# A hybrid decoder layer on one core: the projections' operands at other places in SBUF

## The chip, the cores and the metric

The kernel runs on one core of a Trainium2 chip. The metric is the device time of one execution in microseconds. A core has TensorE (PE in the profile; PEld is its loading of weights), VectorE (DVE), ScalarE (ACT), GpSimd (POOL), SyncE (SP), which here issues nearly all DMAs, and 16 DMA engines. Tiles lie in SBUF, 128 partitions wide; a tile has the same byte address in each partition. A matmul loads a stationary operand of up to 128 columns from SBUF (the LDWEIGHTS of the profile) and then streams a moving operand of up to 512 columns from SBUF, adding into a tile in PSUM. The next matmul's stationary operand is loaded while the current one streams.

## What is computed

One decoder layer for 512 positions of width 1024, in float32, with x and all weights in DRAM:

```python
h = rms_norm(x, norm_w)
u_s, z_s, q, k, v, z_a, r_s, r_a = split(h @ w_in)          # 1024 x 9216
y_s = s5_branch(u_s, ...)                                   # diagonal state space, GELU,
                                                            # gated by sigmoid(g @ w_glu)
y_s = (y_s * silu(z_s)) @ w_ssm_out
y_a = dilated_attention(rope(rms_norm(q)), rope(rms_norm(k)), v)   # 3 groups x 8 heads of 64
y_a = (y_a * silu(z_a)) @ w_attn_out
m = sigmoid(r_s) * y_s + sigmoid(r_a) * y_a
out = x + m @ w_o
```

## The kernel before

**Three products for one.** Every large product is made of operands split in two: hi is the value in the type float32r, lo the rest. `mm3` (L122, its matmuls are L63 in the profile) adds hi x hi, hi x lo and lo x hi into one PSUM tile `pj`, so 128 rows of contraction take three matmuls. Five activations go through it, all transposed (features on the partitions):

- `hT` (L220), the normalized input, [128, 8, 512] in hi and in lo, against all of `w_in`;
- `gT` (L685), the state-space branch after its GELU, against `w_glu`;
- `yT`, the gated branch, against `w_ssm_out`;
- `aT` (L1081), the gated attention, [128, 2, 4, 512], hi and lo in one tile, against `w_attn_out`;
- `mT`, the merged branches, against `w_o`.

**Units.** `load_w` (L185) brings a block of weights of 128 x 1024 by DMA into `w_raw`; ScalarE makes `w_hi` of it (L108) and VectorE `w_lo` (L110). `cm_unit` (L195) takes such a block as stationary operand, in slices of 128 columns, and streams the activation, 512 columns at a time: 8 x 3 = 24 matmuls. `wide_granule` and `tok_granule` do it the other way round: a slice of 128 positions of the activation is stationary, and 512 or 256 columns of weights are moving. The first three blocks are taken with 256 columns of `hT` at a time. A stationary slice is 128 x 4 = 512 bytes, a moving one 2048 or 1024, and every slice starts at a multiple of 512 bytes into its tile. So the distance between a moving and a stationary operand, modulo 512 bytes, is that of their tiles.

**Order.** The work goes through the norm, the projections that feed the state-space branch with that branch's scan between them, `w_glu`, `w_ssm_out`, four rounds of attention (projections of two heads each, scores, softmax, values), `w_attn_out` and `w_o`. Tile pools place the tiles and a planner orders the instructions of each engine.

**Places.** A pool puts its tiles one behind the other in the order in which the program first asks for them, rounded up to 32 bytes. The pool `cst` comes first (`ident`, `nwc`, then `hT_hi` and `hT_lo`), then `wp` with the weights, then `big`, whose tags s4, s7a, s3, s6a, s2, s7b, s1, s5 and s6b are places that several tiles take one after another. The bytes in a partition, before:

| tile (tag) | address | modulo 512 | distance to the weights |
| --- | --- | --- | --- |
| hT_hi, hT_lo | 17056, 33440 | 160 | 32 below |
| w_hi, w_lo (three each) | 74432 to 94912 in steps of 4096 | 192 | 0 |
| gT_lo, aT (s4) | 99008 | 192 | 0 |
| gT_hi (s3) | 120000 | 192 | 0 |
| yT_lo, mT_lo (s2) | 142528 | 192 | 0 |
| yT_hi, mT_hi (s1) | 163008 | 192 | 0 |

The operands of the scores (`qkp`, hi in s1 and lo in s2) are at 192 modulo 512 too.

Of the kernel before, what the change touches and what calls it, by code (L numbers as in the profile page):

```python
# [11 lines left out]
F32 = mybir.dt.float32  # L12
F32R = mybir.dt.float32r
# [7 lines left out]
P = 128  # L21
D = 1024
S = 512
KT = D // P
NB = S // P
G = 64
N = 64
# [6 lines left out]
NP = 4  # L34
NG = 3
# [17 lines left out]
def tile_hybrid_block(ctx: ExitStack, tc: tile.TileContext, x, positions, norm_w, w_in, lam_re, lam_im,  # L53
# [21 lines left out]
    cst = ctx.enter_context(tc.tile_pool(name="cst", bufs=1))  # L75
    wp = ctx.enter_context(tc.tile_pool(name="wp", bufs=3))
    big = ctx.enter_context(tc.tile_pool(name="big", bufs=1))
# [4 lines left out]
    ps_p = ps_first.enter_context(tc.tile_pool(name="ps_p", bufs=3, space=PSUM))  # L82
    ps_g = ps_first.enter_context(tc.tile_pool(name="ps_g", bufs=5, space=PSUM))

    scr_t = big.tile([P, 4096], F32, name="scr", tag="s4")
    scr_o = [0]

    def scr(shape, dtype=F32):
# [11 lines left out]
    def bank(name):  # L100
        return ps_g.tile([P, 512], F32, name=name, tag="g")
# [103 lines left out]
    nw8 = big.tile([KT, P], F32, name="nw8", tag="s7a")  # L205
    act.dma_start(nw8, norm_w[0].rearrange("(k p) -> k p", p=P))
    nwc = cst.tile([P, KT], F32, name="nwc")
    nps = bank("nps")
    pe.transpose(nps[:, 0:KT], nw8, ident[:KT, :KT])
    dve.tensor_copy(nwc, nps[:, 0:KT])  # L210
# [6 lines left out]
        if r in (1, 2):  # L217
            prefetch(len(loaded) + 1)
    lo_w[0] = dve
    hT_hi = cst.tile([P, KT, S], F32R, name="hT_hi")  # L220
    hT_lo = cst.tile([P, KT, S], F32R, name="hT_lo")

    ss = scr([P, NB])
    ms = scr([P, NB])
# [147 lines left out]
    cs = scr([G, N])  # L372
    sincos(sn, cs, th_, [G, N], "la")

    pw = big.tile([G, 2, 9, N], F32, name="pw", tag="s7a")
    dve.tensor_tensor(pw[:, 0, 0], mag, cs, op=ALU.mult)
    dve.tensor_tensor(pw[:, 1, 0], mag, sn, op=ALU.mult)
    den = scr([G, N])
# [13 lines left out]
    dve.tensor_tensor(t2, nr, li, op=ALU.mult)  # L392
    dve.tensor_tensor(t1, t1, t2, op=ALU.subtract)
    dve.tensor_tensor(pw[:, 1, 8], t1, den, op=ALU.mult)
    tq = big.tile([G, 2, 4, N], F32, name="tq", tag="s7b")
    for n in (1, 2, 4):

        br_ = pw[:, 0:1, n - 1:n, :].broadcast_to([G, 2, n, N])
# [1 line left out]
        a = pw[:, :, 0:n, :]  # L400
# [141 lines left out]
    sp.dma_start(qkw[:, 1].rearrange("p g d -> p (g d)"),  # L542
                 k_norm_w[0].rearrange("g d -> (g d)").unsqueeze(0).to_broadcast([P, NG * HD]))
    dve.tensor_scalar(qkw[:, 0], qkw[:, 0], -0.125, None, op0=ALU.mult)
    wcol = cst.tile([P, NG, 2], F32, name="wcol")
    wps = bank("wcp")
    for g in range(NG):
        for a in range(2):
# [50 lines left out]
            act.copy(V[:, 1:3, 2 * b:2 * b + 2], pss[b].rearrange("p (r g c) -> p g r c", r=2, g=2))  # L599

    def new_v():
        return big.tile([P, NG, NB, P], F32, name="V", tag="s6a")


    scn = big.tile([P, 4096], F32, name="scn", tag="s3")
# [61 lines left out]
    V = None  # L667
    fill = list(order)

    def filler():  # L670
        nonlocal V
        kind, c = fill.pop(0)
        if kind == "v0":
            V = new_v()
            v0_unit(0, V)()
        elif kind == "v":
            v_granule(0, V)
        else:
            {"za": za_unit, "zs": zs_unit, "rs": rs_unit, "ra": ra_unit}[kind](c)
# [3 lines left out]
        wx(*js)  # L683

    gT_hi = big.tile([P, KT, S], F32R, name="gT_hi", tag="s3")  # L685
    gT_lo = big.tile([P, KT, S], F32R, name="gT_lo", tag="s4")
    Mb = [dd[:, o:o + 1024].rearrange("p (g k) -> p g k", g=8) for o in (0, 1024, 2048)]
    for M in Mb:
        pool.memset(M, 0.0)
# [206 lines left out]
    def qk_second(hp, mid=None):  # L896

        pss = wide_granule(hT_hi, hT_lo, mid)
        raw = new_raw(0)
        V = new_v()  # L900
        sq = sml.tile([P, NB, 8], F32, name="ssq")[:, :, 0:4]
        for r in range(NB):
            act.copy(raw[:, r], pss[r][:, 0:256])
            squares(sq[:, r], pss[r][:, 0:256])
            act.copy(V[:, 1:3, r], pss[r][:, 256:512].rearrange("p (g c) -> p g c", g=2))  # L905
        qk_norm((2,), [raw], sq)
        return raw, V
# [170 lines left out]
    QK = (QT, KA, KB)  # L1078
    ptb = big.tile([P, 4, 512], F32, name="ptb", tag="s6b")
    PT = [ptb[:, i] for i in range(4)]  # L1080
    aT = big.tile([P, 2, NP, S], F32R, name="aT", tag="s4")  # L1081

    raws = qk_first()

# [9 lines left out]
    for hp in range(NP):  # L1094
        Pt = scores(hp, *QK)
        if hp < NP - 1:
# [12 lines left out]
            V = V_next  # L1109
# [18 lines left out]
    for cc in range(KT // 2):  # L1128
        hi, lo = get_w()
        for c2 in range(2):  # L1130
            c = 2 * cc + c2
# [50 lines left out]
```

## Time and profile before

| | us |
| --- | --- |
| three runs | 736.49, 738.57, 737.64 |
| median | 737.64 |
| profiled execution: span from the first instruction to the last | 732.6 |
| VectorE busy | 457.1 |
| ScalarE busy | 314.6 |
| GpSimd busy | 191.7 |

The profiled execution is given by its span alone; the median of the runs is 5.0 us above it, for what lies before the first and behind the last instruction. The page lists the busy time of each engine, the span in 40 slices, the chain of work that ended last (followed back from the last instruction, at each step to what released it) and groups of instructions by line, engine, operation and tile. A row of such a group ends in the busy time of the group, the mean duration of one in ns, and the idle time of the engine before them. A row of the timeline begins with the start of the instruction and its duration in us; where several alike follow each other they are one row with a count. The durations of matmuls overlap, since a matmul starts before the one ahead of it has drained: the time from one start to the next is what a matmul costs the engine.

### The profile page before, as it was taken

The page shows a single profiled execution, that of the slowest core. Times are in us where ns is not written, and L with a number is a line of the kernel's source. Part 1 is how long each engine was busy: PE and PEld are TensorE (multiplying, and loading weights), DVE is VectorE, ACT ScalarE, POOL GpSimd, SP SyncE. Part 2 cuts the span into 40 slices and gives each one's busy share as a digit, 9 for nine tenths or more (in the row PEclk, how much of TensorE's full clock was granted, in tenths as well). Part 3 has the DMA queues.
Part 4 walks back from the last instruction along what each step waited for, and adds up shares of the span by engine and source line. Part 5 has one row for each costly group of instructions (what it writes and reads, how often), then busy time and mean ns, then how long its engine had stood idle before and what let it go on. Part 6 is the DMA issues. An engine that isn't in the chain of part 4 may idle for free.

```text
span 732.6 us, 12680 instructions
## 1 busy us (share of the span) xinstructions
PE 699.6 (95%) x4821; PEld 574.2 (78%) x4821; DVE 457.1 (62%) x912; ACT 314.6 (43%) x631; POOL 191.7 (26%) x346
## 2 busy tenths in 40 slices
PE   2799899999999999999999999999989999999997
PEld 2687688778878787888888888788868877878886
DVE  6759673989946546764335659655664666464832
ACT  6434463332326465442144456537153734443420
POOL 3426540230205343550000316021601250230000
PEclk9999999999999999999999999999999999999999
DMA  8433653564547554455333432222412231326441
GB/s 203 106 96 94 171 144 77 137 149 132 120 131 153 122 103 133 139 168 172 99 100 87 130 87 79 66 58 58 115 31 79 65 89 30 115 73 236 139 144 57
DMA packets 137213, 82.14 MB, mean 112 GB/s; under 512 B 32696, under 2 KB 125632, under 8 KB 137024
## 3 DMA queue, kind: packets, MB, share of 16 engines
q1 hardware_dynamic: 135088, 78.96, 37.5%
q0 software_dynamic: 2048, 2.36, 2.6%
q8 instruction: 38, 0.62, 0.4%
q14 instruction: 23, 0.19, 0.1%
q10 hardware_dynamic: 16, 0.00, 0.0%
HBM read 68.46 MB, written 10.49 MB: 108 GB/s over the span
## 4 chain that ended last, share of the span: by engine, by line
PE 87%; DMA 4%; ACT 3%; DVE 3%; SPq 2%; issue 1%; ACTq 0%
PE pj L63 71%; DMA w_raw<-in_w_in_dram 3%; PE sps L63 3%; PE yps L63 3%; PE ot L63 2%; PE ptp L67 2%; PE kps L63 2%; PE xps L63 1%; PE qtp L67 1%; DMA Uj<-ud 1%; ACT w_hi L108 1%; SPq L442 1%; PE wps L67 1%; ACT qkp L873 1%; DVE w_lo L110 1%
## 5 line engine op out<-in xcount | busy, mean ns | idle before, releaser
L108 ACT ACTIVATE w_hi<-w_raw 128x1024 fp32r<-128x1024 f32 x100 | 106.0, 1061 | 236.8 <-PE pj L63 206.6
L110 DVE TENSOR_TENSOR w_lo<-w_raw,w_hi 128x1024 fp32r<-128x1024 f32 x98 | 124.3, 1268 | 107.9 <-ACT w_hi L108 107.2
L63 PE MATMUL pj<-hT_lo,w_hi 128*128 128x512 f32 (+1 forms) x344 | 132.9, 387 | 3.0 <-DVE hT_lo L251 3.0
L63 PE MATMUL pj<-hT_hi,w_hi 128*128 128x512 f32 (+1 forms) x344 | 132.8, 389 | 2.4 <-ACT V L905 1.4
L63 PE MATMUL pj<-hT_hi,w_lo 128*128 128x512 f32 (+1 forms) x344 | 132.4, 386 | 1.6 <-DVE w_lo L110 1.6
L63 PE MATMUL pj<-w_hi,hT_hi 128*128 128x512 f32 (+1 forms) x288 | 106.5, 372 | 0.0
L63 PE MATMUL pj<-w_lo,hT_hi 128*128 128x512 f32 (+1 forms) x288 | 106.5, 370 | 0.0
L63 PE MATMUL pj<-w_hi,hT_lo 128*128 128x512 f32 (+1 forms) x288 | 106.0, 371 | 0.0
L63 PEld LDWEIGHTS pj<-hT_lo,w_hi 128*128 128x128 f32 x344 | 66.0, 192 | 16.2 <-DVE hT_lo L251 3.9
L63 PEld LDWEIGHTS pj<-hT_hi,w_hi 128*128 128x128 f32 x344 | 65.5, 192 | 16.5 <-ACT V L905 2.1
L63 PEld LDWEIGHTS pj<-hT_hi,w_lo 128*128 128x128 f32 x344 | 65.9, 192 | 15.4 <-DVE w_lo L110 2.3
L63 PEld LDWEIGHTS pj<-w_hi,hT_hi 128*128 128x128 f32 x288 | 54.1, 188 | 10.0 <-issue 0.2
L63 PEld LDWEIGHTS pj<-w_hi,hT_lo 128*128 128x128 f32 x288 | 54.0, 188 | 10.0
L63 PEld LDWEIGHTS pj<-w_lo,hT_hi 128*128 128x128 f32 x288 | 54.0, 188 | 9.8
L931 ACT ACTIVATE Pt<-Pt,st 128x256 f32<-128x256 f32 (+1 forms) x64 | 31.0, 492 | 18.7 <-DVE st L929 18.7
L735 POOL TENSOR_TENSOR kt<-kt,dg 16x128 f32<-16x128 f32 x8 | 4.6, 571 | 125.0 <-ACT kt L734 118.4
L852 POOL TENSOR_TENSOR rt<-qraw,tC 128x256 f32<-128x256 f32 x12 | 14.3, 1189 | 87.7 <-DVE qraw L846 87.4
L739 POOL DMA_DIRECT2D dd<-kt x64 | 33.7, 535 | 2.4 <-POOL kt L735 2.4
L874 DVE SCALAR_TENSOR_TENSOR qkp<-qtp,wcol,qkp 128x512 fp32r<-128x512 f32 (+1 forms) x32 | 23.0, 745 | 13.5 <-ACT qkp L873 13.4
L961 POOL COPY sw<-st 32x4 f32<-32x4 f32 x64 | 12.0, 187 | 73.2 <-ACT Pt L931 70.5
L873 ACT ACTIVATE qkp<-qtp,wcol 128x512 fp32r<-128x512 f32 (+1 forms) x32 | 20.8, 685 | 15.7 <-PE qtp L67 10.4
L277 POOL TENSOR_TENSOR ab<-dd,AT 128x512 f32<-128x512 f32 x16 | 23.0, 1446 | 11.6 <-DVE ab L278 11.6
(263 smaller groups left out, 1289.4 us busy)
## 6 DMA issues: line engine op xcount, KB each, us to landing
w_raw<-in_w_in_dram SPq DMA_DIRECT2D x40, 512.0 KB
w_raw<-in_w_in_dram SPq DMA_DIRECT2D x112, 128.0 KB
w_raw<-in_w_glu_dram SPq DMA_DIRECT2D x8, 512.0 KB
w_raw<-in_w_ssm_out_dram SPq DMA_DIRECT2D x8, 512.0 KB
w_raw<-in_w_o_dram SPq DMA_DIRECT2D x8, 512.0 KB
x_all<-in_x_dram SPq DMA_DIRECT2D x4, 512.0 KB
ud<-uT SPq DMA_DIRECT2D x8, 256.0 KB
Uj<-ud SPq DMA_DIRECT2D x8, 256.0 KB
```

What stands on the lines that cost most here:

```text
L63: last[0] = nc.tensor.matmul(*a, **k)
L67: last[0] = nc.tensor.transpose(*a, **k)
L108: act.activation(hi, src, AF.Copy, scale=scale)
L110: e.tensor_tensor(lo, src, hi.bitcast(F32), op=ALU.subtract)
L277: eng.tensor_tensor(tv, a2.unsqueeze(2).broadcast_to(sh), ai, op=ALU.mult)
L442: sp.dma_start(D1[64 * h:64 * h + 64, a], bv[a][h])
L739: pool.dma_start(M[Q * t:Q * t + Q, :, 0:P - Q * t], kt[:, :, t:].rearrange("q g k p -> q g (k p)"))
L852: pool.tensor_tensor(t1, rh[:, :, :, 0:16], cv.broadcast_to([P, NB * 2, 2, 16]), op=ALU.mult)
L873: act.activation(hi, ps[sl], AF.Copy, scale=w)
L874: dve.scalar_tensor_tensor(lo, ps[sl], w, hi.bitcast(F32), op0=ALU.mult, op1=ALU.subtract)
L931: act.activation(o, o, AF.Exp, bias=nm, scale=-1.0, accum_out=st[:, kind, 1, h, b:b + 1])
L961: pool.tensor_copy(sw[32 * r:32 * r + 32, :, :, b], st[32 * b:32 * b + 32, 1, :, :, r])
```

## The change

No operation is added, removed or put elsewhere in the program. `wcol`, a tile of 24 bytes in `cst`, is asked for ahead of `hT_hi` and not behind `maskB`; so `hT` begins 32 bytes higher and all that follows in `cst` ends where it did. In `big` the tiles of four tags ask for 128, 128, 64 and 64 bytes more (s4, s7a, s6a, s7b); those of s4 use what lies behind the first 128 bytes, the others leave the end unused. So the places behind them move up.

```diff
+    def offset(shape, dtype, name, tag, pad):
+
+        n = int(np.prod(shape[1:]))
+        v = big.tile([P, pad + n], dtype, name=name, tag=tag)[:, pad:]
+        if len(shape) == 3:
+            v = v.rearrange("p (a b) -> p a b", b=shape[2])
+        elif len(shape) == 4:
+            v = v.rearrange("p (a b c) -> p a b c", b=shape[2], c=shape[3])
+        return v
+
-    scr_t = big.tile([P, 4096], F32, name="scr", tag="s4")
+    scr_t = offset([P, 4096], F32, "scr", "s4", 32)
...
     nwc = cst.tile([P, KT], F32, name="nwc")
+    wcol = cst.tile([P, NG, 2], F32, name="wcol")
+    hT_hi = cst.tile([P, KT, S], F32R, name="hT_hi")
+    hT_lo = cst.tile([P, KT, S], F32R, name="hT_lo")
...
-    pw = big.tile([G, 2, 9, N], F32, name="pw", tag="s7a")
+    pw = big.tile([G, 2 * 9 * N + 32], F32, name="pw", tag="s7a")[:, 0:2 * 9 * N].rearrange("g (a k n) -> g a k n", a=2, k=9)
...
-    tq = big.tile([G, 2, 4, N], F32, name="tq", tag="s7b")
+    tq = big.tile([G, 1024 + 16], F32, name="tq", tag="s7b")[:, 0:512].rearrange("g (a k n) -> g a k n", a=2, k=4)
...
-        return big.tile([P, NG, NB, P], F32, name="V", tag="s6a")
+        return big.tile([P, NG * NB * P + 16], F32, name="V", tag="s6a")[:, 0:NG * NB * P].rearrange("p (g b c) -> p g b c", g=NG, b=NB)
...
-    gT_lo = big.tile([P, KT, S], F32R, name="gT_lo", tag="s4")
+    gT_lo = offset([P, KT, S], F32R, "gT_lo", "s4", 32)
...
-    aT = big.tile([P, 2, NP, S], F32R, name="aT", tag="s4")
+    aT = offset([P, 2, NP, S], F32R, "aT", "s4", 32)
```

The places that follow from these sizes:

| tile (tag) | address | modulo 512 | distance to the weights |
| --- | --- | --- | --- |
| hT_hi, hT_lo | 17088, 33472 | 192 | 0 |
| w_hi, w_lo | as before | 192 | 0 |
| gT_lo, aT (s4) | 99136 | 320 | 128 |
| gT_hi (s3) | 120256 | 448 | 256 |
| yT_lo, mT_lo (s2) | 142848 | 0 | 320 |
| yT_hi, mT_hi (s1) | 163392 | 64 | 384 |

The other tiles of `big`, and the pools `tmp` and `sml` behind it, move by 64 to 384 bytes. The operands of the scores lie 64 bytes modulo 512 apart between hi and lo.

More of the change, by code (lines that the diff above doesn't have):

```diff
@@ L219, in tile_hybrid_block @@
     lo_w[0] = dve
-    hT_hi = cst.tile([P, KT, S], F32R, name="hT_hi")
-    hT_lo = cst.tile([P, KT, S], F32R, name="hT_lo")
     ss = scr([P, NB])
@@ L544, in tile_hybrid_block @@
     dve.tensor_scalar(qkw[:, 0], qkw[:, 0], -0.125, None, op0=ALU.mult)
-    wcol = cst.tile([P, NG, 2], F32, name="wcol")
     wps = bank("wcp")
```

## The prediction

> **What bounds the kernel now.** I read the page first, from the busy times to the chain of work that ended last.
>
> ```profile
> span 732.6 us, 12680 instructions
> PE 699.6 (95%) x4821; PEld 574.2 (78%) x4821; DVE 457.1 (62%) x912; ACT 314.6 (43%) x631; POOL 191.7 (26%) x346
> PEclk9999999999999999999999999999999999999999
> PE 87%; DMA 4%; ACT 3%; DVE 3%; SPq 2%; issue 1%; ACTq 0%
> ```
>
> TensorE is busy for 95% of the span, at practically its full granted clock, and 87% of the chain is its own work. So the end of the kernel moves with the time from one matmul's start to the next one's. The chain's shares by line and the window of all instructions that touch the tile pj say which matmuls those are:
>
> ```profile
> by line: PE pj L63 71.3%; DMA w_raw<-in_w_in_dram 2.6%; PE sps L63 2.6%; PE yps L63 2.6%; PE ot L63 2.1%; PE ptp L67 1.9%; PE kps L63 1.7%; PE xps L63 1.3%; PE qtp L67 1.0%; DMA Uj<-ud 1.0%; ACT w_hi L108 0.9%; SPq L442 0.9%; PE wps L67 0.9
> 0.00:733.00 733.00, 576.83 (x2568) 457.43 (x2568) 24.35 (x36) 64.28 (x138) 0.99 0.41 112
> ```
>
> In the second row stand the window, its length, then busy time and (count) of TensorE. The 2568 projection matmuls (pj) are 71.3% of the chain. The groups of TensorE kept apart by shape count them by operand. Each row is one of three products that mm3 issues, except aT, whose row and the one after it hold two and one:
>
> ```profile
> L63 PE MATMUL pj<-hT_hi,w_hi 128*128 128x512 f32 x296 | 118.8, 401 | 1.4 <-ACT V L905 1.4
> L63 PE MATMUL pj<-w_hi,hT_hi 128*128 128x512 f32 x224 | 88.6, 398 | 0.0
> L63 PE MATMUL pj<-gT_hi,w_hi 128*128 128x512 f32 x64 | 24.7, 391 | 1.0 <-ACT gs L776 1.0
> L63 PE MATMUL pj<-yT_hi,w_hi 128*128 128x512 f32 x64 | 24.9, 389 | 0.0
> L63 PE MATMUL pj<-w_hi,mT_hi 128*128 128x512 f32 x64 | 24.4, 389 | 0.0
> L63 PE MATMUL pj<-aT,w_hi 128*128 128x512 f32 x64 | 19.9, 393 | 0.0
> L63 PE MATMUL pj<-w_hi,hT_hi 128*128 128x256 f32 x64 | 18.0, 281 | 0.0
> L63 PE MATMUL pj<-aT,w_lo 128*128 128x512 f32 x32 | 12.4, 392 | 0.0
> L63 PE MATMUL pj<-hT_hi,w_hi 128*128 128x256 f32 x48 | 14.0, 312 | 1.0 <-ACT w_hi L108 1.0
> ```
>
> So hT takes part in 3 x (296 + 224) = 1560 matmuls of 512 columns and 3 x (48 + 64) = 336 of 256. The other four operands have 3 x 64 x 3 + 96 = 672, all of 512. Their mean durations are 389 to 393 ns, hT's 398 to 401. These durations overlap; what the chain pays is the distance between starts, and the timeline of TensorE gives it. First and last rows of four unbroken runs (hT moving, 15 steps; hT stationary, 15; gT, 15; mT stationary, 15):
>
> ```profile
> 168.07 0.40 PE L63 MATMUL pj<-hT_hi,w_lo 128*128 128x512 f32 x1
> ...
> 171.57 0.40 PE L63 MATMUL pj<-hT_hi,w_lo 128*128 128x512 f32 x1
> ...
> 378.38 0.39 PE L63 MATMUL pj<-w_hi,hT_hi 128*128 128x512 f32 x1
> ...
> 381.88 0.40 PE L63 MATMUL pj<-w_hi,hT_hi 128*128 128x512 f32 x1
> ...
> 305.86 0.39 PE L63 MATMUL pj<-gT_hi,w_lo 128*128 128x512 f32 x1
> ...
> 309.26 0.39 PE L63 MATMUL pj<-gT_hi,w_lo 128*128 128x512 f32 x1
> ...
> 710.11 0.39 PE L63 MATMUL pj<-w_hi,mT_hi 128*128 128x512 f32 x1
> ...
> 713.51 0.39 PE L63 MATMUL pj<-w_hi,mT_hi 128*128 128x512 f32 x1
> ```
>
> With hT 3.50 us / 15 = **233.3 ns**, in either role. With gT and mT 3.40 us / 15 = **226.7 ns**, in either role. Same shape, same type, same clock, no wait between. What differs in the program is the place: before, hT begins 32 bytes off the weights' place modulo 512, and gT, yT, mT and aT begin at it. Every slice of these tiles and of the weights that a matmul takes starts at a multiple of 512 bytes into its tile, so a distance modulo 512 holds for all of a stage's matmuls.
>
> **The change part by part.** No instruction, DMA or wait is added or removed; only addresses move. The weights stay where they are, so no queue gets a new step.
>
> *hT to distance 0.* The nearest row for the new distance is gT's and mT's 226.7 ns. Per matmul 233.3 - 226.7 = 6.67 ns, times 1560 = 10.4 us. Two deductions. First, distance 0 doesn't give 226.7 at once. This is the start of the aT stage, just behind the last hT matmuls:
>
> ```profile
> 655.61 0.63 PE L63 MATMUL pj<-aT,w_hi 128*128 128x512 f32 x2
> 656.08 0.39 PE L63 MATMUL pj<-aT,w_lo 128*128 128x512 f32 x1
> ...
> 656.77 0.39 PE L63 MATMUL pj<-aT,w_lo 128*128 128x512 f32 x1
> ...
> 657.45 0.39 PE L63 MATMUL pj<-aT,w_lo 128*128 128x512 f32 x1
> ...
> 658.13 0.39 PE L63 MATMUL pj<-aT,w_lo 128*128 128x512 f32 x1
> ```
>
> From 655.61 to 656.77 are five gaps, 232 ns each; from 657.45 on it is 226.7 (0.68 / 3). Five gaps at 5.3 ns too much cost 27 ns after each break in the stream. The hT matmuls make 65 units of 24 (1560 / 24), and I take one break per unit, as the chain shows two neighbouring ones here with the state-space work between:
>
> ```profile
> 222.15 7.23 PE pj L63 x31
> 229.38 0.32 PE kps L63 x4
> ...
> 234.33 7.23 PE pj L63 x31
> ```
>
> 65 x 27 ns = 1.7 us, leaving 8.7. Second, what isn't on the chain brings nothing: pj holds 0.713 x 732.6 = 522 us of the chain, and its starts add up to 1560 x 233.3 + 336 x 116.7 + 672 x 226.7 ns = 555 us, so 0.94 of it counts: **8.2 us**. The cover that takes the rest is the wait for weights and for the first stages' data, in the 732.6 - 699.6 = 33 us in which TensorE is idle: there a faster matmul only waits earlier.
>
> *hT's 256-column matmuls.* The timeline of such a run (18 steps) and of one at the kernel's start (9 steps), the granted clock of the latter's window (0.50), and the timeline of ten score matmuls with the row that follows them:
>
> ```profile
> 187.19 0.28 PE L63 MATMUL pj<-w_hi,hT_hi 128*128 128x256 f32 x1
> ...
> 189.29 0.28 PE L63 MATMUL pj<-w_hi,hT_hi 128*128 128x256 f32 x1
> ...
> 36.77 0.41 PE L63 MATMUL pj<-hT_hi,w_hi 128*128 128x256 f32 x1
> ...
> 38.69 0.41 PE L63 MATMUL pj<-hT_hi,w_hi 128*128 128x256 f32 x1
> ```
>
> ```profile
> 36.80:38.60 1.80, 1.80 (x10) 0.50 0.00 0
> ```
>
> ```profile
> 435.82 1.36 PE L63 MATMUL sps<-qkp 128*128 128x256 f32 x10
> 437.02 0.39 PE L63 MATMUL pj<-w_hi,hT_hi 128*128 128x512 f32 x1
> ```
>
> They step at 2.10 / 18 = 116.7 ns. At distance 0 the trace has only the scores (sps), ten in 1.20 us, 120 ns; half of the 512-column gap would be 113.3. Bounds 336 x (-3.4 to +3.3 ns), -1.1 to +1.1 us; I take 0.
>
> *gT, yT, mT, aT away from distance 0.* The new distances are 128 (aT, gT_lo), 256 (gT_hi), 320 (yT_lo, mT_lo) and 384 (yT_hi, mT_hi). No row shows these. The best end is a column per clock. Half clock shows 1.92 us / 9 = 213.3 ns for 256 columns, so full clock would give 213.3 for 512: 672 x 13.4 ns = 9.0 us gained. The worst end among the rows is the first pair of aT, 655.61 to 656.08, 235 ns each: 672 x 8.3 = 5.6 us lost. Between them I take **0**. 512- and 256-column matmuls with hT carry the same surcharge per column (20 ns on 213.3, 10 ns on 106.7), which looks like a stall that recurs every few columns, so like a short period in the address. 32 bytes off costs, and the new distances are all multiples of 64. Cover there is none: these stages are pure TensorE, and any loss or gain is paid whole.
>
> *Everything else that moves* (the score operands, now 64 bytes apart between hi and lo; the scan's, tmp and small tiles): the sps share of 2.6% bounds it to well under 1 us either way; taken as 0.
>
> The Trainium skill speaks against the first term. Its page "TensorE: Matmul & The Clock Gate", section "Step-by-step: what each phase is for", says that TensorE reads moving operand and weights through two independent SBUF ports, so that loading the next weights takes nothing from the running matmul. By that the sum would be 0 and the time 737.6. The trace doesn't agree, as far as 233.3 and 226.7 ns can tell. The same page's section "Back-to-back issue gap" gives N / 2.4 + 2.5 ns, an estimate of 215.8 for 512 columns; no row here reaches it, and if the new distances did, the four operands would gain an estimated 7.3 us.
>
> Sum: -10.4 + 1.7 + 0.5 (off the chain) + 0 + 0 = -8.2 us. The span would be 732.6 - 8.2 = 724.4. Against the median of the three runs, 737.64, which lies 5.0 above the span for what is around it, that gives **729.4 us**.
>
> **The rivals.**
>
> 1. *The place isn't why hT is slower.* For: the kernel has one hT only, so tile and place can't be told apart. Against: hT costs 233.3 as moving and as stationary operand, and both hi and lo, as a place would. Time: 737.6. Chance 0.07.
> 2. *Distance 0 is special, and the four others now pay what hT paid.* For: 32 bytes off cost 6.67 ns, and the other distances are unseen. Against: the short period. 672 x 6.67 = 4.5 us back: 733.9. Chance 0.22.
> 3. *Some new distance is better than 0.* For: 226.7 is still 13.4 above the 213.3. Half of that on all four operands: 4.5 us more, 724.9. Chance 0.12.
> 4. *Slower.* The two streams meet at one of the new distances at every fetch, where at distance 0 they soon slip past each other (232 falling to 226.7). From a gap of 226.7 + 8.2 us / 672 = 239 ns on, the four operands eat the gain, and from 242 it is a measurable loss. At three times the surcharge of distance 0, 213.3 + 40 = 253.3 ns, they lose 17.9 us: 747.3. Against: no steady or passing gap in these rows exceeds 235. Chance 0.05.
>
> **How the numbers follow.** The forecast, hT at 226.7 and the others unchanged, has 0.54. A measurement of this kernel tells about 0.3% (2.2 us) from no change, so faster means under 735.4. All of the forecast, rival 3 and most of rival 2 are faster: 0.83. Rival 1 and the worse part of 2 are within: 0.12. Rival 4 is slower: 0.05. The range leaves out rival 4, rival 1 and the extreme of rival 3: from 723, where half the possible gain of the four others meets the whole 256-column one, to 735.5, where they pay 235 ns.
>
> **What would show it.** In the changed kernel's timeline hT's unbroken runs step by 226.7 ns; if they stay at 233.3, rival 1 holds. The gaps of gT, yT, mT and aT, read by hi and lo, decide between the forecast and rivals 2 to 4, each at its own distance. The 256-column runs step by 113 to 120. The chain's share of pj falls while the waits for w_lo and Uj grow by under 1 us. The forecast is wrong if the order of instructions differs, or if idle time of TensorE grows by more than that.

## The result: 5.8 us less

| | median, us | lowest to highest | runs |
| --- | --- | --- | --- |
| before | 736.28 | 734.70 to 738.57 | 7 |
| changed | 730.48 | 729.30 to 733.67 | 7 |

The ratio is 0.992, with a 95% interval of 0.9901 to 0.994: 4.4 to 7.3 us less. The forecast was 729.4.

The page of the changed kernel shows its slowest execution of the seven (own time 733.67, span 731.9):

```profile
span 731.9 us, 12680 instructions
PE 698.2 (95%) x4821; PEld 577.0 (79%) x4821; DVE 454.6 (62%) x912; ACT 314.6 (43%) x631; POOL 189.8 (26%) x346
PEclk9999899999999999999999999999999999999999
PE 89%; ACT 3%; DMA 3%; SPq 2%; DVE 2%; issue 0%; ACTq 0%
```

The 8 in the row of the granted clock goes with its being the slowest: its mean clock is 0.988, that of the other six 0.992 or 0.993, and their spans are 727.5 to 728.9. So a total of this page isn't held against one of before's page; the distances between starts are, read where the clock is full. The number of instructions is the same on every engine, and TensorE's come in the same order.

The timeline of the changed kernel gives those distances (start, duration, instruction). First and last rows of unbroken runs: hT moving, 15 steps; hT's 256 columns, 21; gT, 15; mT, 15; aT, 12:

```profile
158.37 0.39 PE L63 MATMUL pj<-hT_hi,w_hi 128*128 128x512 f32 x1
...
161.77 0.39 PE L63 MATMUL pj<-hT_hi,w_hi 128*128 128x512 f32 x1
...
187.94 0.28 PE L63 MATMUL pj<-w_hi,hT_hi 128*128 128x256 f32 x1
...
190.46 0.28 PE L63 MATMUL pj<-w_hi,hT_hi 128*128 128x256 f32 x1
...
305.99 0.39 PE L63 MATMUL pj<-gT_hi,w_hi 128*128 128x512 f32 x1
...
309.46 0.40 PE L63 MATMUL pj<-gT_hi,w_hi 128*128 128x512 f32 x1
...
709.84 0.39 PE L63 MATMUL pj<-w_hi,mT_hi 128*128 128x512 f32 x1
...
713.29 0.39 PE L63 MATMUL pj<-w_hi,mT_hi 128*128 128x512 f32 x1
...
674.98 0.39 PE L63 MATMUL pj<-aT,w_lo 128*128 128x512 f32 x1
...
677.77 0.39 PE L63 MATMUL pj<-aT,w_lo 128*128 128x512 f32 x1
```

hT steps by 3.40 / 15 = 226.7 ns, its 256 columns by 2.52 / 21 = 120.0; gT by 3.47 / 15 = 231.3, mT by 3.45 / 15 = 230.0 and aT by 2.79 / 12 = 232.5. So hT got what the four others had, and the four others got most of what hT had. Over all unbroken starts (gaps under 250 ns, or 128 for 256 columns) the means in ns are these; they include the first matmuls behind a break:

| matmuls | before | changed | hT alone moved | the four alone moved |
| --- | --- | --- | --- | --- |
| hT, 512 columns (1560) | 233.2 | 227.9 | 227.7 | 233.2 |
| hT, 256 columns (336) | 117.3 | 119.8 | 119.8 | 117.6 |
| gT (192) | 226.8 | 231.4 | 227.0 | 229.3 |
| yT (192) | 226.7 | 231.6 | 226.7 | 232.2 |
| mT (192) | 226.7 | 230.2 | 226.7 | 230.3 |
| aT (96) | 227.3 | 232.5 | 227.0 | 232.5 |

The last two columns belong to the first experiments.

### The profile page after: what moved, and what is told of

Read it like the earlier page. It is cut to its first block, busy times and chain, and to the rows that moved or that the text cites. A ratio compares the mean times of both kernels' runs of the same rounds, so it can differ in the third digit from the quotient of the medians.

```text
span 731.9 us, 12680 instructions
## 1 busy us (share of the span) xinstructions
PE 698.2 (95%) x4821; PEld 577.0 (79%) x4821; DVE 454.6 (62%) x912; ACT 314.6 (43%) x631; POOL 189.8 (26%) x346
## 4 chain that ended last, share of the span: by engine, by line
PE 89%; ACT 3%; DMA 3%; SPq 2%; DVE 2%; issue 0%; ACTq 0%
PE pj L63 73%; PE sps L63 3%; PE yps L63 3%; PE ot L63 2%; PE ptp L67 2%; PE kps L63 2%; DMA w_raw<-in_w_in_dram 1%; PE xps L63 1%; DMA Uj<-ud 1%; PE qtp L67 1%; SPq L453 1%; PE wps L67 1%; ACT qkp L883 1%; ACT w_hi L118 1%; DVE w_lo L120 1%; SPq L229 1%
## 5 line engine op out<-in xcount | busy, mean ns | idle before, releaser
L63 PE MATMUL pj<-gT_hi,w_hi 128*128 128x512 f32 x64 | 25.0, 396 | 1.0 <-ACT gs L786 1.0
```

Source lines behind the costliest of these rows:

```text
L63: last[0] = nc.tensor.matmul(*a, **k)
```

## The experiments

**The change in two halves.** Theory: only the distance between a moving and a stationary operand counts, so the two halves have opposite signs. Rival: the halves don't matter by distance, and the gain comes from elsewhere, or from both. Three kernels on one chip, with before at 734.72 (733.13 to 736.24, 11 runs). The changed kernel once more:

> The changed kernel again, beside the next two on the same chip. Distance theory (a matmul's price depends on the distance between moving operand and weights modulo 512 bytes, 0 being the cheapest seen): hT's 512-column gaps 226.7 ns, the other four 230 to 232.5, together 4 us less than before, ratio about 0.994. If the first comparison's 0.992 holds, 730 us.

Only `wcol` and `hT` moved in `cst`; gT, yT, mT and aT stay at distance 0:

```diff
     nwc = cst.tile([P, KT], F32, name="nwc")
+    wcol = cst.tile([P, NG, 2], F32, name="wcol")
+    hT_hi = cst.tile([P, KT, S], F32R, name="hT_hi")
+    hT_lo = cst.tile([P, KT, S], F32R, name="hT_lo")
...
-    hT_hi = cst.tile([P, KT, S], F32R, name="hT_hi")
-    hT_lo = cst.tile([P, KT, S], F32R, name="hT_lo")
...
-    wcol = cst.tile([P, NG, 2], F32, name="wcol")
```

> hT at distance 0, the other four left at distance 0. Distance theory: hT's gaps 226.7 ns, gT, yT, mT and aT 226.7 as before, so the 3 us that the four lost come back: 7 us less than before, ratio 0.990, and 3 us under the changed kernel. Rival (the four stages got slower because of something other than their distance, such as hT's new place): they stay at 230 to 232 and the time equals the changed kernel's.

The other half alone: the changed kernel with this edit taken back, so hT stays 32 below the weights and the four lie at 128 to 384:

> hT left 32 bytes below the weights, the other four moved as in the change. Distance theory: hT's gaps 233.3 ns as before, the four at 230 to 232.5, 3 us more than before, ratio 1.004. Rival (the four gain or lose nothing on the chain): ratio 1.000.

| | median, us | ratio to before | 95% interval |
| --- | --- | --- | --- |
| the whole change | 729.23 (726.76 to 733.90) | 0.9931 | 0.9906 to 0.9955 |
| hT alone | 728.01 (724.35 to 730.56) | 0.9905 | 0.9882 to 0.9928 |
| the four alone | 738.90 (736.49 to 741.52) | 1.0058 | 1.0038 to 1.0079 |

The window of all instructions that touch pj, in this order, one row from each kernel's trace (window, length, TensorE's busy time and count; then the other engines, granted clock, DMA):

```profile
0.00:733.00 733.00, 572.48 (x2568) 458.45 (x2568) 24.37 (x36) 64.27 (x138) 0.99 0.40 112
```

```profile
0.00:733.00 733.00, 570.37 (x2568) 459.23 (x2568) 24.37 (x36) 64.26 (x138) 0.99 0.40 112
```

```profile
0.00:733.00 733.00, 579.35 (x2568) 457.57 (x2568) 24.36 (x36) 64.24 (x138) 0.99 0.40 112
```

Against the 576.83 of before: hT alone -6.46, the four alone +2.52, and the whole -4.35, which is about their sum (-3.94). So one half of the change brings the gain and the other takes back a third or more of it. hT alone is the better kernel by medians, by 1.2 us where 3 were expected, and its interval overlaps that of the whole change.

**Which distances cost.** The forecast took the new distances to be free because they are multiples of 64. This kernel (from hT alone) gives every load of weights another place, in steps of 32 bytes over 512, hi and lo alike, so all distances occur in one trace. Two buffers of `tmp` pay for the room.

```diff
-        hi = wp.tile([P, kts, cols], F32R, name="w_hi", tag="w_hi")
-        lo = wp.tile([P, kts, cols], F32R, name="w_lo", tag="w_lo")
+        o = 8 * (n_load[0] % 16)
+        n_load[0] += 1
+        hi, lo = (wp.tile([P, 1024 + 128], F32R, name=t, tag=t)[:, o:o + 1024].rearrange("p (k c) -> p k c", k=kts)
+                  for t in ("w_hi", "w_lo"))
```

> All five activations at one place modulo 512, and each block of weights, hi and lo, at 0, 32, 64 ... 480 bytes from it, in turn from load to load; tmp has four buffers instead of six, so only the gaps inside a block of 24 matmuls are read, not the time. Distance theory: each distance has its own steady gap, 226.7 at 0, 230 to 232.5 at 128, 256, 320 and 384, 233.3 where the moving operand lies 32 below (or, with weights moving, 32 above). Rival (only the alignment to 64 bytes matters): two values alone, 226.7 at multiples of 64 and 233.3 at odd multiples of 32.

One execution, 739.29 us. Its timeline in the stage of yT, each row the start of a block of 24 matmuls, with the distance (activation minus weights) falling from 160 by 32 to 0, and the start behind the last block:

```profile
342.01 0.39 PE L63 MATMUL pj<-yT_hi,w_hi 128*128 128x512 f32 x1
...
347.63 0.39 PE L63 MATMUL pj<-yT_hi,w_hi 128*128 128x512 f32 x1
...
353.20 0.40 PE L63 MATMUL pj<-yT_hi,w_hi 128*128 128x512 f32 x1
...
358.80 0.40 PE L63 MATMUL pj<-yT_hi,w_hi 128*128 128x512 f32 x1
...
364.30 0.40 PE L63 MATMUL pj<-yT_hi,w_hi 128*128 128x512 f32 x1
...
369.90 0.39 PE L63 MATMUL pj<-yT_hi,w_hi 128*128 128x512 f32 x1
...
375.34 0.40 PE L63 MATMUL pj<-w_hi,hT_hi 128*128 128x512 f32 x1
```

The blocks take 5.62, 5.57, 5.60, 5.50, 5.60 and 5.44 us, so 234.2, 232.1, 233.3, 229.2, 233.3 and 226.7 ns a matmul for 160, 128, 96, 64, 32 and 0. The means over all blocks with hT moving, without the first six matmuls behind a break or a change of distance and without the last of a block:

| distance | 0 | 32 | 64 | 96 | 128 | 160 | 192 | 224 |
| --- | --- | --- | --- | --- | --- | --- | --- | --- |
| ns | 226.9 | 233.3 | 228.6 | 233.5 | 232.2 | 234.4 | 233.3 | 233.3 |
| distance | 256 | 288 | 320 | 352 | 384 | 416 | 448 | 480 |
| ns | 226.7 | 233.3 | 228.8 | 233.5 | 233.4 | 234.3 | 233.6 | 233.3 |

The second half repeats the first within 0.3 ns, but for 128 and 384 (1.2): the period is 256 bytes. Of these distances 0 and 256 are free, 64 and 320 cost some 2 ns, all others 5 to 8. So neither the short period nor "a multiple of 64" holds: 128 and 192 are multiples of 64 and pay almost all. The expected 230 to 232.5 at 256 and 320 fell too. The sign counts: 64 is cheap and 192, which is -64, is not. The table gives the address of the moving operand minus that of the stationary one. Where hT is stationary the same trace shows the same values (228.4 at 64, 233.3 at 192), so for an activation that is stationary the distance turns round: 320 from the weights counts as 192, and pays.

**Distance or place.** If the place of each operand by itself counted (its alignment, say), hT alone would be fast because 192 modulo 512 is a good place. Here, from hT alone, `wcol` grows so that hT, the weights and the four all move to 288 modulo 512, an odd multiple of 32:

```diff
-    wcol = cst.tile([P, NG, 2], F32, name="wcol")
+    wcol = cst.tile([P, 30], F32, name="wcol")[:, 0:6].rearrange("p (g a) -> p g a", a=2)
```

> hT, the weights and the four others all at one place again, but at 288 modulo 512 (192 in hT_only), an odd multiple of 32. Distance theory: 226.7 ns for all of them and hT_only's time, ratio 0.990. Rival (192 or 448 modulo 512, or a multiple of 64, is a good place in itself): gaps of 233.3 ns, about 15 us more than hT_only, ratio 1.01.

And from hT alone, the four moved by one whole period, to distance 256 (`offset` is the function of the change):

```diff
-    scr_t = big.tile([P, 4096], F32, name="scr", tag="s4")
+    scr_t = offset([P, 4096], F32, "scr", "s4", 64)
...
-    gT_lo = big.tile([P, KT, S], F32R, name="gT_lo", tag="s4")
+    gT_lo = offset([P, KT, S], F32R, "gT_lo", "s4", 64)
...
-    aT = big.tile([P, 2, NP, S], F32R, name="aT", tag="s4")
+    aT = offset([P, 2, NP, S], F32R, "aT", "s4", 64)
```

> hT at distance 0, gT, yT, mT and aT all at distance 256 in hi and lo. Period of 256 bytes, as the probe in steps of 32 showed on hT: gaps of the four 226.7 ns, ratio 0.990 as hT_only. Rival (256 isn't free for these tiles; gT_hi, at 256 in the changed kernel, had 231.5): about 231 ns, 3 us more, ratio 0.994.

On one chip, before at 735.91 (732.02 to 737.65, 11 runs): the first 729.44 us, ratio 0.991 (0.9883 to 0.9936), the second 727.92 us, ratio 0.9892 (0.9868 to 0.9916). An unbroken run of hT in the first and of gT in the second, 15 steps each:

```profile
158.12 0.39 PE L63 MATMUL pj<-hT_hi,w_hi 128*128 128x512 f32 x1
...
161.52 0.39 PE L63 MATMUL pj<-hT_hi,w_hi 128*128 128x512 f32 x1
```

```profile
306.24 0.39 PE L63 MATMUL pj<-gT_hi,w_hi 128*128 128x512 f32 x1
...
309.64 0.39 PE L63 MATMUL pj<-gT_hi,w_hi 128*128 128x512 f32 x1
```

Both 3.40 / 15 = 226.7. The place 288, an odd multiple of 32, is as good as 192 if both operands share it, and 256 is as good as 0. It is the distance that counts. In the changed kernel gT_hi lies at 256, so what gT pays there should come with its lo half at 128. With the four alone moved this can be read off: by the time stamps of that trace, without the first six behind a break, the gap behind a matmul that streams gT_lo is 233.6 ns (62 of them), behind one that streams gT_hi 227.2 (gT_lo streams next) and 226.8 (gT_hi again; 59 each). In the changed kernel, at the same distances, all three are long (230.1, 231.4 and 232.5).

**Below 32 bytes.** The same probe in steps of 4 bytes (`o = 1 * (n_load[0] % 16)`), to see whether distances inside one line of 16 bytes are free:

> All five activations at one place and each block of weights, hi and lo, at 0, 4, 8 ... 60 bytes from it, in turn; tmp has four buffers, so only gaps are read. If what counts is which line of 16 bytes is read, 4, 8 and 12 give 226.7 ns as 0 does, and 16 on 233.3. If 32-byte lines count, up to 28 give 226.7. Rival (any other distance than an exact 0 costs): 233.3 from 4 on. A gap under 226.7 at one of them would be a better place than 0.

One execution, 738.0 us. Timeline, starts of blocks of 24 at distances -4, -8, -12 and -16, and the start behind them:

```profile
155.10 0.39 PE L63 MATMUL pj<-hT_hi,w_hi 128*128 128x512 f32 x1
...
160.68 0.39 PE L63 MATMUL pj<-hT_hi,w_hi 128*128 128x512 f32 x1
...
166.22 0.39 PE L63 MATMUL pj<-hT_hi,w_hi 128*128 128x512 f32 x1
...
171.73 0.39 PE L63 MATMUL pj<-hT_hi,w_hi 128*128 128x512 f32 x1
...
177.33 0.28 PE L63 MATMUL pj<-w_hi,hT_hi 128*128 128x256 f32 x1
```

5.58, 5.54, 5.51 and 5.60 us, so 232.5, 230.8, 229.6 and 233.3 ns. Four bytes off already cost most of the surcharge; the expectation of a free line fell. With the weights moving, +4 gave the highest mean of all, 237.4, while +28 and +60 were nearly free (227.8 and 227.9). No distance of this probe has a mean under 226.7, though single gaps of 225 alternate with 235 at -12.

**Half of the loads displaced.** The 32-byte probe with w_hi left at distance 0 and only w_lo moving (one of every three matmuls uses w_lo):

```diff
-        hi, lo = (wp.tile([P, 1024 + 128], F32R, name=t, tag=t)[:, o:o + 1024].rearrange("p (k c) -> p k c", k=kts)
-                  for t in ("w_hi", "w_lo"))
+        hi, lo = (wp.tile([P, 1024 + 128], F32R, name=t, tag=t)[:, i:i + 1024].rearrange("p (k c) -> p k c", k=kts)
+                  for t, i in (("w_hi", 0), ("w_lo", o)))
```

> The hi half of each block of weights at distance 0, the lo half at 0, 32 ... 480 in turn; tmp has four buffers. In a block with hT moving the three products are (moving hi on w_hi), (lo on w_hi), (hi on w_lo). If the price comes from the loading of the next weights beside the running matmul, the second, during which w_lo is loaded, changes; if it comes from a matmul's own weights, the third. If the matmuls' phases carry over, all three change, and the mean of the three stays between 226.7 and 233.3.

One execution, 737.48 us. Timeline, block starts with hT at the distances 480, 448 and 416 from w_lo (w_lo 32, 64 and 96 bytes further up), and the start behind them:

```profile
159.15 0.39 PE L63 MATMUL pj<-hT_hi,w_hi 128*128 128x512 f32 x1
...
164.74 0.40 PE L63 MATMUL pj<-hT_hi,w_hi 128*128 128x512 f32 x1
...
170.30 0.39 PE L63 MATMUL pj<-hT_hi,w_hi 128*128 128x512 f32 x1
...
175.88 0.39 PE L63 MATMUL pj<-hT_hi,w_hi 128*128 128x512 f32 x1
```

5.59, 5.56 and 5.58 us, so 232.9, 231.7 and 232.5 ns on average, although only a third of the loads is displaced. Which of the three products is long differs by distance: at 384 they take 227, 232.5 and 234 ns, at 480 they take 233, 239 and 228. A displaced third costs nearly as much as displacing all, but this run can't tell which matmul pays, since the next third begins before the stream has settled.

**Which matmul pays.** So, from the kernel just shown, the units that stream an activation over a block of weights (`cm_unit`) are regrouped: first the 16 matmuls with w_hi, then the 8 with w_lo, so that the stream settles within each group. The weights lie 0, 32, ... 224 bytes further up than the activation in turn, w_lo in one kernel and w_hi in its mirror, in which w_lo stays at 0. In this part "at 32" means 32 bytes further up, which is 224 (256 - 32) in the table above.

```diff
-        o = 8 * (n_load[0] % 16)
+        o = 8 * (n_load[0] % 8)
...
         for k in range(kts):
-            mm3(ps, hi[:, k], lo[:, k], rh[:, k], rl[:, k], k == 0, k == kts - 1)
+            pe.matmul(ps, hi[:, k], rh[:, k], start=k == 0, stop=False, skip_group_check=True)
+            pe.matmul(ps, hi[:, k], rl[:, k], start=False, stop=False, skip_group_check=True)
+        for k in range(kts):
+            pe.matmul(ps, lo[:, k], rh[:, k], start=False, stop=k == kts - 1, skip_group_check=True)
```

> In the units that stream the activation over a block of weights the 24 matmuls are regrouped: first the 16 that use w_hi, then the 8 that use w_lo; w_hi lies at distance 0 from the activation, w_lo at 0, 32, ... 224 bytes in turn. Theory A (the stream collides with the load of the next stationary operand): the 16th matmul, which itself uses w_hi but during which the first w_lo slice is loaded, is the first whose gap leaves 226.7 ns, and the 24th, which uses w_lo while a w_hi slice is loaded, is the first to be back on its way to 226.7. Theory B (what counts is the place of the stationary operand that the matmul itself uses): the 16th still takes 226.7, the 17th is the first to be longer, the 24th is still long. At w_lo distance 0 all 24 take 226.7 after settling. The time is about 731 to 738 us, since a third of those units' matmuls and all others with w_lo stay displaced.

> The same regrouped units, with w_lo at distance 0 and w_hi at 0, 32, ... 224 bytes in turn, so 16 displaced matmuls and then 8 that are not. Theory A (collision with the next load): the 16th, during which the first w_lo slice at distance 0 is loaded, is already near 227, and the 24th, during which the next unit's w_hi is loaded, is already long. Theory B (the matmul's own stationary operand): the 16th is still long, the 17th is the first on its way to 226.7, the 24th is 226.7 and the first of the next unit is the first long one.

One execution each, 729.9 us (731 to 738 was expected) and 733.76 beside 733.79 of before. The gaps in ns from each start to the next, in single units, from the traces' time stamps; the bars set off the 16th, the last one with w_hi, and the 24th:

```
w_hi at 0, w_lo at 32 (unit at 329.12):
  226 227 227 226 227 227 226 227 227 226 227 227 226 227 227 | 235 | 230 230 235 231 235 232 235 | 232
w_hi at 0, w_lo at 224 (unit at 357.60):
  236 228 232 231 227 227 226 227 227 226 227 227 226 227 227 | 235 | 233 234 231 235 233 234 231 | 227
mirror, w_hi at 224, w_lo at 0 (unit at 360.85):
  234 234 231 235 233 234 231 235 233 235 230 235 234 234 231 | 226 | 227 226 227 227 226 227 227 | 227
mirror, both at 0, the next unit's w_hi at 32 (unit at 322.10):
  227 226 227 227 226 227 227 226 227 227 226 227 227 226 227 | 227 | 226 227 227 226 227 227 226 | 235
```

The 16th matmul decides. In the first two units its own stationary operand is w_hi at distance 0, and it is long; what isn't at 0 is the operand that is being loaded for the one behind it. The fourth unit shows the same with hi and lo exchanged: 24 matmuls at distance 0, and the last is long because the next block's w_hi lies at 32. The third unit fits as well: its 16th has its own operand at 224 and is short. But that way round is seldom so clean, as told below. The timelines of TensorE and of its weight loads around the 16th matmul of the first unit (which starts at 329.12 + 15 x 0.227 = 332.52):

```profile
332.29 0.39 PE L63 MATMUL pj<-yT_hi,w_hi 128*128 128x512 f32 x1
332.52 0.40 PE L63 MATMUL pj<-yT_lo,w_hi 128*128 128x512 f32 x1
332.76 2.02 PE L63 MATMUL pj<-yT_hi,w_lo 128*128 128x512 f32 x8
```

```profile
332.30 0.19 PEld L63 LDWEIGHTS pj<-yT_lo,w_hi 128*128 128x128 f32 x1
332.52 0.88 PEld L63 LDWEIGHTS pj<-yT_hi,w_lo 128*128 128x128 f32 x4
```

The load of the first w_lo slice starts at 332.52, with the 16th matmul, and runs beside it. So the price of the distance is paid while the activation streams and the next stationary operand is loaded. The 16th is long in all 22 units at 32, 128, 160 and 224 in which the two gaps before it were 228 ns or less: 235 at 32 and at 224, 232 or 233 at 128, 236 or 237 at 160. At 96 it is 228 or 229, and at 64 and 192 (6 units) it is 225 or 226 and the first long one is the 17th. By themselves those would fit theory B too; beside the others it looks as if the collision took a matmul to build up there. In the mirror, the 24th in front of a displaced w_hi has the same values at each of these distances (12 units at the same four). A matmul whose own operand lies at 0 is long, so theory B falls.

The way back is less clear. The expected quick return was seen at 224 in the first kernel, where the 24th is 226 or 227 in all six units, and in three of the mirror's seven units at 224 (226 or 227 for the 16th, the third unit shown among them). At all other distances the matmul in front of the return still takes 229 to 240 ns, and a stream back at distance 0 needs up to nine more to settle (236 228 232 231, then 227, in the second unit shown). Both theories allow that, so the case against B rests on the way in. And hi and lo of the activation lie at one place here, so these two kernels can't tell whether the load meets the operand that streams beside it or the one that streams next. gT with the four alone moved speaks for the one beside it: behind gT_hi (256 from the weights) with gT_lo (128) next the gap is 227.2, behind gT_lo with gT_hi next 233.6. That is one trace; in the changed kernel the three gaps don't come apart like this.

## The prediction, step by step

- **hT to distance 0** was right, and so was its cause: 233.3 to 226.7 exactly as quoted. Settling costs (227.9 - 226.7) x 1479 unbroken starts = 1.8 us, priced 1.7. At the other 81 starts there was nothing to gain (0.5 us), and with hT alone moved the gaps at breaks grew from 29.7 to 30.7 us. All 1560 starts together went from 375.75 to 368.22 us, 7.5 less where 8.2 was summed.
- **hT's 256-column matmuls** came out at the upper bound of their gap, 120 ns, not unchanged: (119.8 - 117.3) x 298 unbroken starts = 0.7 us lost. The score matmuls, the only row with distance 0, had been the right one to go by.
- **gT, yT, mT and aT: the step that failed.** It took 0, "the new distances are all multiples of 64" and "a short period in the address". The runs show 230.2 to 232.5 ns and a period of 256 bytes; of the new distances only 256 is free, 320 is cheap for yT, which streams, and not for mT, which is stationary, and hi and lo of no tile lie both at those. The starts of the four add up to 152.98 us before and 155.94 in the second run of the changed kernel: 3.0 us lost. What the runs showed in place of 0 is rival 2, with two thirds of its price (4.5). The form of the surcharge, so many ns per column, said nothing about its period in the address: that was a guess, and the range covered it.
- **Everything else** stayed small. In the second run of the changed kernel the span is 5.3 us shorter than before's and pj 4.35. The largest part of the remainder is in the transposes of the probabilities (ptp, L67), whose busy time was 18.78 us before, 17.64 in this run and 19.67 in the changed kernel's first profile: it varies between executions of one kernel, so it isn't put down to the change. It goes with the granted clock: from 604 to 608 us, within these transposes, that is 0.71 before, 1.00 in the second run and 0.64 in the first profile.
- **The wait for Uj** was to grow by under 1 us. It went from 3.4 us to 4.5 on the page of the changed kernel and 3.5 in the second run; the wait for w_lo stayed at 1.6. The share of pj on the chain was to fall. It rose to 73.5% on that page and stayed at 71.3% in the second run: the weights' DMA has 2.6% of the chain before and 1.4% and 2.0% here, so the way that the chain takes near the start seems to outweigh 4 us; that is argued, not shown.
- **Around the span** the forecast took 5.0 us. Every run of the changed kernel lies 1.8 above its span (733.67 - 731.9, 730.48 - 728.7). The 5.0 was 1.8 and a profile of an execution quicker than the median. Besides, the median of before over seven runs was 736.28, not 737.64. So the forecast's 729.4 owes some of its closeness to luck, a starting point 1.4 us high, while the change gave 5.8 where 8.2 was summed. The ends of the range, too, come out of their terms as 729.4 - 4.5 - 1.1 = 723.8 and 729.4 + 5.6 = 735.0, not 723 and 735.5.
- **The Trainium skill's rule** (page "TensorE: Matmul & The Clock Gate", section "Step-by-step: what each phase is for"), that the load of the next weights takes no read bandwidth from the running matmul, doesn't hold for these matmuls. The regrouped units show a gap of 235 in place of 227 ns by the place of the weights being loaded and nothing else. It holds at distances 0 and 256 only as far as 226.7 ns can tell.
- **Rival 1** (place isn't the cause) falls with hT alone and with all tiles shifted together; **rival 3** (a better distance than 0) with the two probes, where the mean of 512 columns goes under 226.7 at none; **rival 4** as a whole, since no stage's mean at the new distances came near 239 (232.5 is the highest; single gaps reach 241), though half of the change by itself is slower than before.

What remains open: what in the memory or the read path makes 256 bytes the period, and why 64 is nearly free and -64 isn't. The runs show that loading and streaming collide, not where. Part of the gain of 5.8 us, about 1.5 us beyond pj's 4.35, is inside the interval and wasn't traced to a place.

## What to carry to other kernels

Where TensorE bounds a kernel and matmuls of one shape follow each other without a wait, read the distance from start to start by operand: a difference of 3% at the same clock may be nothing but an address. Put moving and stationary tiles of such float32r matmuls, both halves of a split one, at the same place modulo 256 bytes, and see that a small tile ahead of them in a pool doesn't shift all that follows. A change that moves several tiles is best taken apart tile by tile: here moving one was worth some 7 us, and moving the others cost 3 us by the starts and 1 to 4 by the times (728.01 to 729.23, 734.72 to 738.90).

## What the runs showed that was not expected

- One distance can have two steady rhythms. At -12 bytes one block took 229.6 ns a matmul and another 233.4; gT at the same distances took 231.4 in the changed kernel and 229.3 with the four alone moved. What decides between them wasn't tested.
- 256-column matmuls have their best distance elsewhere: some 115 ns at 448 (192 modulo 256) in the 32-byte probe and 120 at 0 in the changed kernel, where 512 columns are best.
- The spread between executions of one kernel goes with the granted clock: the seven of the changed kernel have 733.67 us at 0.988 and 729.3 to 730.71 at 0.992 to 0.993. That is over half of what the change brought, so the gaps between starts told more than one execution's time.
